# Where the weight buffers of the second expert stage lie, and which step lets the third expert's weights be fetched

## The chip, the cores and the metric

The kernel runs on one core of a Trainium2 chip. The metric is device microseconds of one launch; the span of a profile is the time from its first to its last instruction on that core.

## The reference

A two-layer model: each layer is a mixer followed by a mixture of experts. The changed code is the expert part and the seam between it and the mixer in front of it.

```python
DEPTH = 2
MOE_EXPERTS = 32          # 4 groups of 8
MOE_TOP_K = 2
MOE_FF = D_MODEL // 2     # 512, D_MODEL = 1024

for l in range(DEPTH):
    ...                                        # norm, modulation, mixer: even for l = 0, odd for l = 1
    x = x + mod_l[2][:, None] * y_l            # out projection of the mixer, residual
    h2_l = rms_norm(x, norm_w[l, 1]) * (1.0 + mod_l[4][:, None]) + mod_l[3][:, None]
    ...                                        # l = 0: 256 context tokens and 512 others; l = 1: 512
    y2 = hierarchical_moe(h2, wg, bg, we, be, w1, w3, w2)

# hierarchical_moe: a group, then the two best experts of it for each token; for each expert
#   y = (silu(x @ w1[e]) * (x @ w3[e])) @ w2[e]
# scaled by its gate and added up for each token
```

Every expert has three float32 matrices of 2 MB: w1 and w3 (1024x512) and w2 (512x1024). The 32 experts of a stage are 192 MB, and the two stages read 384 MB.

## The kernel before

The order on the core is: even mixer, expert stage l = 0 (768 tokens, "first stage"), odd mixer, expert stage l = 1 (512 tokens, "second stage"), final norm.

**The seam.** `mix_out` (L663) does the out projection of the mixer in 128-token tiles, four for l = 1 and six for l = 0. For each tile it loads the residual (tile `oxr`, SP's queue), runs two groups of matmuls into `po`, adds, stores `xmid`, computes the normed rows, stores them to DRAM as `h2d` (POOL's queue), and routes the tile's tokens. The last matmul of tile n's out projection is kept as `s.marks[n]` (in the order in which tiles are done), the second residual load as `s.oxr1`. Behind the last tile the routing builds the tables `ixm`, which say for each expert which rows to gather. The residual tiles and the routing's work tiles (pools `mob` and `mow`) are memory that is in use until those tables are done.

**An expert stage.** `moe` (L890) handles expert e in iteration e and e + 1: POOL gathers its token rows (`hga`, and `hgb` for an overflow block), PE transposes them (`xt`), multiplies by w1 and w3 (`pa`, 16 matmuls of the program, 32 in the trace), transposes the gated product (`gt`) and multiplies by w2 (`ya`); POOL scatters the result to `yd`. For the overflow block there are `pb` and `yb`; PE reads a flag of the expert from memory (`values_load` of `fl`, L1003, a TENSOR_LOAD) and branches to the real block or to one short matmul with zeros. All 32 flags of a stage are read by PE's own queue, at places that the scheduler picks.

**The weights.** All weight loads go through `wdma` (L950) in one chain on SP's queue, 1 MB each. I number these pieces of a stage from 0: pieces 0 to 3 are w2 of experts 0 and 1; 4 to 7, 8 to 11 and 12 to 15 are w1 and w3 of experts 0, 1 and 2; 16 to 19 those of expert 3, 20 to 23 of expert 4; then six for each expert, beginning with w2 of expert 2 (24 and 25), of expert 3 (30 and 31), and so on, so that w2 of expert 8 begins with piece 60. SP's queue runs in order: a piece that waits holds all that stands behind it, residual loads too.

Two things hold a piece. The first is its memory: `load13` takes buffers of 2 MB (two pieces each) from seven in turn, `load2` takes its two pieces from a ring of four 1 MB buffers, which w2 of the expert before the last has to leave first (its `yb` is the last reader). The seven buffers are pools that are opened at the right end of memory, `rb` first, then `ra`, and what they overlie depends on that. In the built program of the second stage one of the seven, byte 81,888 of each partition, overlies the routing's work tiles (`mob`, `mow`); the six from 98,272 on overlie memory that the mixer itself has left by then. The one over the routing is the first in turn. The second thing is pacing: the list `ahead` says for the first pieces which `marks` entry each has to wait for, and the two pieces after the list wait for `gathers[3]`, the fourth gather.

Of the kernel before, what the change touches and what calls it, by code (L numbers as in the profile page):

```python
# [8 lines left out]
F32 = mybir.dt.float32  # L9
# [73 lines left out]
class Kern:  # L83
# [806 lines left out]
    def moe(s, l):  # L890
# [6 lines left out]
        yv = [s.yd[l][:2 * ntok].rearrange("t (h n) -> (t h) n", h=m) for m in (2, 4)]  # L897
        with ExitStack() as es:
            rb = es.enter_context(s.pool(f"ringb{l}", bufs=(2, 3)[l], side="right"))
            ra = es.enter_context(s.pool(f"ringa{l}", bufs=4, side="right"))  # L900
            rc = es.enter_context(s.pool(f"ringc{l}", side="right")) if l == 0 else rb
            mp = es.enter_context(s.pool(f"moe{l}"))
            wk = es.enter_context(s.pool(f"moew{l}", bufs=2))
            pst = es.enter_context(s.pool(f"moet{l}", bufs=2, psum=True))
# [11 lines left out]
            scat, turn, chain, gathers = [], [0], [], []  # L916


            ahead = [-1, -1, -2, -2] + [[0, 0, 1, 1, 2, 2, 3, 3, 5, 5], [0, 0, 0, 1, 1, 1, 2, 2, 3, 3]][l]

            def columns(e):

# [22 lines left out]
            def at(wv, e, k0, k1):  # L945
                if isinstance(e, int):
                    return wv[e, :, k0:k1]
                return wv[bass.ds(e, 1), :, k0:k1].rearrange("a p k n -> (a p) k n")

            def wdma(e, dst, src):  # L950
                x = nc.sync.dma_start(dst, src)
                if isinstance(e, int):
                    if chain:
                        s.pace(x, chain[-1], False)

                    if len(chain) < len(ahead):
                        if ahead[len(chain)] >= 0:
                            s.pace(x, s.marks[ahead[len(chain)]])
                        elif ahead[len(chain)] == -2:
                            s.pace(x, s.oxr1, True)  # L960
                    elif len(chain) < len(ahead) + 2:
                        s.pace(x, gathers[3])
                    chain.append(x)

            def load13(e):
                r = []
                for a in range(2):
                    t = (ra, ra, ra, ra, rb, rb, rc)[turn[0] % 7].tile([128, 2, 4, 512], F32, name="mw")
                    turn[0] += 1
                    for i, wv in enumerate((w1, w3)):  # L970
                        wdma(e, t[:, i], at(wv, e, 4 * a, 4 * a + 4))
                    r.append(t)
                return r
# [55 lines left out]
            def gxpose(g):  # L1029
                t = pst.tile([128, 512], F32, tag="t", name="gt")  # L1030
                for c in range(3):
                    nc.tensor.transpose(t[:, c * 128:(c + 1) * 128], g[:, c * 128:(c + 1) * 128], s.ident)  # L1032
                gT = wk.tile([128, 384], F32, name="gT")
                nc.vector.tensor_copy(gT, t[:, :384])
                return gT
# [34 lines left out]
            if l == 1:  # L1070

                m5a, m5b = mp.tile([128, 512], F32, name="m5a"), mp.tile([128, 256], F32, name="m5b")
                for t, m in ((m5a, 2), (m5b, 4)):
                    n = D // m
                    for i in range(m):
                        src = s.modd[1][2][4 + 2 * (i * n // 512):5 + 2 * (i * n // 512), i * n % 512:i * n % 512 + n]
                        s.pace(nc.gpsimd.dma_start(t[128 // m * i:128 // m * (i + 1)], src.to_broadcast([128 // m, n])), gathers[3], False)
            w2t = [load2(0), load2(1)]
            w13 = [load13(0), load13(1), load13(2)]
            xs = {0: [xpose(0, 0), xpose(0, 1)]}  # L1080
            g, pb, yb, gT = {}, {}, {}, {}
            for e in range(NE + 1):
                if e < NE:
                    if e + 2 < NE:
                        gather(e + 2, columns(e + 2))
                    if 0 < e < NE - 2:
                        w13.append(load13(e + 2))
                    if e > 1:
                        w2t.append(load2(e))
# [26 lines left out]

            if l == 1:
                big = lambda pool: pool.tile([128, 2, 4, 512], F32, name="mw").rearrange("p a b c -> p (a b c)")
                fin = s.final_load(big(ra), big(ra))
            else:  # L1120
                s.vraw = s.vload(0)

            with tc.For_i(0, nov, 1) as o:  # L1123
                cols = []
                for ix, gt in s.R["otab"]:
                    c = wk.tile([128, 2], I32, name="ocol")
                    nc.vector.tensor_copy(c[:, 0:1], ix[:, 0, bass.ds(o, 1)])
                    nc.vector.tensor_copy(c[:, 1:2], ix[:, 1, bass.ds(o, 1)])
                    g = wk.tile([128, 1], F32, name="ogate")
                    nc.vector.tensor_copy(g, gt[:, bass.ds(o, 1)])  # L1130
                    cols.append((c[:, 0:1], c[:, 1:2], g))
                e = nc.values_load(s.R["oi"][0:1, bass.ds(o, 1)], engines=[mybir.EngineType.SP], min_val=0, max_val=NE - 1)
                gather(NE, cols)
                w, wd = load13(e), load2(e)
                pa = up_a(w, xpose(NE, 0))
                xb, p = xpose(NE, 1), pbt()
                up_b(p, w, xb)
                gg = wk.tile([128, 384], F32, name="gg")
                gate(gg, pa, 0, 256)
                gate(gg, p, 256, 128)  # L1140
                t = gxpose(gg)
                down_a(wd, t, cols)
                p = ybt()
                down_b(p, wd, t)
                tail_b(p, cols)
# [322 lines left out]
```

## Time and profile before

| | us |
|---|---|
| median of 3 runs | 2089.74 |
| lowest and highest | 2088.02, 2091.30 |
| the profiled execution | 2089.85 |
| its span | 2088.1 |
| first expert stage, from its first gather | about 510 to 1010 |
| odd mixer | about 1010 to 1465 |
| out projection and routing of l = 1 | about 1465 to 1534 |
| second expert stage | about 1534 to 2045 |
| final norm | about 2045 to 2088 |

PE is busy 1802.3 us of the span (86%) and the weight loads, 384 transfers of 1024 KB, make up most of the 567.73 MB that the DMA engines move. The mean granted clock is 0.963. Shares over the whole span mix stages with different limits, so the stretches have to be read one by one: in the page's slices the DMA row is at 9 in both expert stages and low in the mixers and at the seam between them.

### The profile page before, as it was taken

Reading aid. Unit: us, or ns where it says so; the run is one execution under the profiler, and the core shown is the slowest. Engines: PE = TensorE matmul, PEld = TensorE weight load, DVE = VectorE, ACT = ScalarE, POOL = GpSimd, SP = SyncE. Lnnn points to the kernel's source line nnn. Section 1 sums busy time; section 2 is a strip of 40 time slices with the busy share of each in tenths; the row PEclk is TensorE's granted clock in tenths of the full one; section 3 lists DMA queues with packets and bytes.
Section 4 is the critical chain, followed back from the end, with each engine's and each line's share of the span. In section 5 each row is a group of like instructions: output and inputs, shape, how many; then the busy total and the mean of one; then the engine's idle time right before and its main releaser. Section 6 shows DMA issues by size and latency. Waiting matters only on the chain. (4 is left out here: it accounts for less than half of the span.)

```text
span 2088.1 us, 26462 instructions
## 1 busy us (share of the span) xinstructions
PE 1802.3 (86%) x10109; PEld 843.4 (40%) x10109; DVE 869.0 (42%) x1823; ACT 563.3 (27%) x929; POOL 353.3 (17%) x400
## 2 busy tenths in 40 slices
PE   5999999996989999888589999999959888888882
PEld 2564444453333333233234566556533333333320
DVE  5476455578111111111273796777851212111113
ACT  4355356511111111111243554654210000000000
POOL 2000000013322222211230000000132223222213
PEclk9999999998999999999889999999969999999996
DMA  9515556574999999999773130110469999999996
GB/s 318 202 54 194 193 173 206 183 284 165 410 410 363 412 412 410 410 412 414 298 256 81 41 81 24 61 61 21 175 244 409 411 410 410 410 411 410 410 397 231
DMA packets 168718, 567.73 MB, mean 272 GB/s; under 512 B 21702, under 2 KB 69311, under 8 KB 130659
## 3 DMA queue, kind: packets, MB, share of 16 engines
q1 hardware_dynamic: 145632, 523.88, 65.1%
q0 software_dynamic: 22640, 41.30, 5.6%
q8 instruction: 127, 2.08, 0.4%
q14 instruction: 45, 0.36, 0.0%
q10 hardware_dynamic: 274, 0.10, 0.0%
HBM read 554.59 MB, written 39.91 MB: 285 GB/s over the span
## 5 line engine op out<-in xcount | busy, mean ns | idle before, releaser
L144 PE MATMUL pa<-mw,xa 128*64 128x512 f32 x2048 | 537.0, 608 | 28.9 <-DMA mw<-in_moe_w 24.6
L144 PE MATMUL ya<-mw,gT 128*64 128x512 f32 x1024 | 283.8, 602 | 2.3 <-DMA mw<-in_moe_w 1.5
L144 PEld LDWEIGHTS pa<-mw,xa 128*64 128x64 f32 x2048 | 158.4, 139 | 284.1 <-issue 277.4
L144 PE MATMUL px<-hTh,wsh 128*128 128x512 f16 (+1 forms) x672 | 227.1, 339 | 7.5 <-DVE t L438 2.8
L144 PE MATMUL px<-hTl,wsh 128*128 128x512 f16 (+1 forms) x672 | 227.3, 338 | 2.7 <-DVE hTl L348 2.6
L144 PE MATMUL px<-hTh,wsl 128*128 128x512 f16 (+1 forms) x672 | 226.9, 338 | 0.0
L144 PEld LDWEIGHTS <-wsh 128*128 128x128 f16 x1344 | 131.2, 98 | 118.9 <-issue 22.8
L1027 DVE TENSOR_TENSOR gg<-gg,pa 128x256 f32<-128x256 f32 x64 | 26.9, 420 | 332.3 <-ACT gg L1026 332.3
L937 POOL DMA_INDIRECT yd<-sb,ixm x64 | 66.0, 1032 | 583.3 <-DVE sb L1062 293.7
L144 PEld LDWEIGHTS ya<-mw,gT 128*64 128x64 f32 x1024 | 79.3, 136 | 114.4 <-issue 98.3
L1027 DVE TENSOR_TENSOR gg<-gg,pb 128x128 f32<-128x128 f32 x64 | 18.4, 288 | 254.5 <-ACT gg L1026 252.3
L1026 ACT ACTIVATE gg<-pa 128x256 f32<-128x256 f32 x64 | 24.6, 384 | 360.5 <-PE pa L144 360.5
L1026 ACT ACTIVATE gg<-pb 128x128 f32<-128x128 f32 x64 | 17.7, 277 | 277.3 <-PE pb L144 277.3
L138 DVE SCALAR_TENSOR_TENSOR wsl<-w,wsh 128x2048 f16<-128x2048 f32 x34 | 77.8, 2289 | 35.4 <-ACT wsh L135 31.5
L1032 PE MATMUL gt<-cca,gg 128*128 128x128 f32 x192 | 46.5, 306 | 50.5 <-DVE gg L1027 50.5
L144 PEld LDWEIGHTS <-wsl 128*128 128x128 f16 x672 | 66.3, 99 | 51.4 <-issue 6.0
L927 POOL DMA_INDIRECT hga<-h2d,ixm x64 | 66.9, 1045 | 101.7 <-PE xt L987 75.7
L1032 PEld LDWEIGHTS gt<-cca,gg 128*128 128x128 f32 x192 | 21.5, 141 | 147.5 <-DVE gg L1027 98.8
L144 PE MATMUL adaps<-adaw,cT 128*32 128x512 f32 x384 | 75.7, 633 | 4.5 <-DMA adaw<-in_ada_w 3.4
L992 ACT ACTIVATE xa<-xt 128x512 f32<-128x512 f32 x64 | 38.2, 597 | 140.3 <-PE xt L987 137.9
L937 POOL DMA_INDIRECT yd<-sa,ixm x64 | 64.3, 1005 | 69.2 <-ACT sa L1046 31.3
L144 PE MATMUL pv<-wsh,hTh 128*128 128x512 f16 (+1 forms) x192 | 69.0, 360 | 5.8 <-ACT hTh L1227 5.8
(391 smaller groups left out, 2761.5 us busy)
## 6 DMA issues: line engine op xcount, KB each, us to landing
mw<-in_moe_w SPq DMA_DIRECT2D x384, 1024.0 KB
adaw<-in_ada_w SPq DMA_DIRECT2D x40, 1024.0 KB
w<-in_od_w_in SPq DMA_DIRECT2D x32, 512.0 KB
adaw<-in_ada_w SPq DMA_DIRECT2D x16, 512.0 KB
w<-in_ev_w_in SPq DMA_DIRECT2D x8, 1024.0 KB
cy<-yd SPq DMA_DIRECT2D x12, 512.0 KB
xmid<-oxr POOLq DMA_DIRECT2D x10, 512.0 KB
h2d<-ohp POOLq DMA_DIRECT2D x10, 512.0 KB
```

What stands on the lines that cost most here:

```text
L138: i = s.nc.vector.scalar_tensor_tensor(lo, v, WS, hi, op0=ALU.mult, op1=ALU.subtract)
L144: return s.nc.tensor.matmul(ps, lhsT, rhs, start=first, stop=last)
L927: i = nc.gpsimd.indirect_dma_start(out=hg[e % NG][g], out_offset=None, in_=hv[g], in_offset=bass.IndirectOffsetOnAxis(ap=cols[g][0], axis= ...
L937: i = nc.gpsimd.indirect_dma_start(out=yv[g], out_offset=bass.IndirectOffsetOnAxis(ap=cols[g][1], axis=0), in_=yt, in_offset=None, bounds_ ...
L992: nc.scalar.activation(x, v, AF.Copy)
L1026: nc.scalar.activation(g[:, c0:c0 + n], p[:, :n], AF.Silu)
L1027: nc.vector.tensor_tensor(g[:, c0:c0 + n], g[:, c0:c0 + n], p[:, n:2 * n], op=ALU.mult)
L1032: nc.tensor.transpose(t[:, c * 128:(c + 1) * 128], g[:, c * 128:(c + 1) * 128], s.ident)
```

## The change

In the second stage the buffers are split otherwise: `ra` has three, `rb` three, and a pool `rc` of its own holds the seventh. `rc` is opened last, lies at byte 81,888 over the routing's tiles, and comes last in turn; the six buffers before it, 12 pieces, lie on memory that the mixer has left. The final loads take `rb` in place of `ra`.

The list `ahead` grows by two entries in both stages. In the first stage pieces 14 and 15 wait for `marks[5]`, the last out-projection matmul, where they waited for the fourth gather, and pieces 16 and 17 now wait for that gather. In the second stage pieces 10 to 15 wait for `marks[3]`, the last out-projection matmul (10 and 11 waited for `marks[2]`, 14 and 15 for the gather), and 16 and 17 for the gather. So all of w1 and w3 of expert 2 is paced by the out projection.

```diff
             rb = es.enter_context(s.pool(f"ringb{l}", bufs=(2, 3)[l], side="right"))
-            ra = es.enter_context(s.pool(f"ringa{l}", bufs=4, side="right"))
-            rc = es.enter_context(s.pool(f"ringc{l}", side="right")) if l == 0 else rb
+            ra = es.enter_context(s.pool(f"ringa{l}", bufs=(4, 3)[l], side="right"))
+
+            rc = es.enter_context(s.pool(f"ringc{l}", side="right"))
+            ring = [ra] * (4, 3)[l] + [rb] * (2, 3)[l] + [rc]
...
-            ahead = [-1, -1, -2, -2] + [[0, 0, 1, 1, 2, 2, 3, 3, 5, 5], [0, 0, 0, 1, 1, 1, 2, 2, 3, 3]][l]
+            ahead = [-1, -1, -2, -2] + [[0, 0, 1, 1, 2, 2, 3, 3, 5, 5, 5, 5], [0, 0, 0, 1, 1, 1, 3, 3, 3, 3, 3, 3]][l]
...
-                    t = (ra, ra, ra, ra, rb, rb, rc)[turn[0] % 7].tile([128, 2, 4, 512], F32, name="mw")
+                    t = ring[turn[0] % 7].tile([128, 2, 4, 512], F32, name="mw")
...
-                fin = s.final_load(big(ra), big(ra))
+                fin = s.final_load(big(rb), big(rb))
```

SP's queue at the seam to the second stage, before; `in_moe_w2` are pieces 0 to 3, and `mw_13321` is the first buffer of expert 0:

```order
L678 DMA oxr_12649<-xres_66 128x1024
L678 DMA oxr_12678<-xres_66 128x1024
L951 DMA mw_13317<-in_moe_w2 128x2x1024
L951 DMA mw_13318<-in_moe_w2 128x2x1024
L678 DMA oxr_12937<-xres_66 128x1024
L678 DMA oxr_13080<-xres_66 128x1024
L951 DMA mw_13321<-in_moe_w1 128x2048
L951 DMA mw_13321<-in_moe_w3 128x2048
L951 DMA mw_13324<-in_moe_w1 128x2048
```

and after, where line numbers are two higher and `mw_13324` is that first buffer:

```order
L678 DMA oxr_12649<-xres_66 128x1024
L678 DMA oxr_12678<-xres_66 128x1024
L953 DMA mw_13320<-in_moe_w2 128x2x1024
L953 DMA mw_13321<-in_moe_w2 128x2x1024
L678 DMA oxr_12937<-xres_66 128x1024
L953 DMA mw_13324<-in_moe_w1 128x2048
L953 DMA mw_13324<-in_moe_w3 128x2048
L678 DMA oxr_13080<-xres_66 128x1024
L953 DMA mw_13327<-in_moe_w1 128x2048
```

Pieces 4 and 5 have moved ahead of the fourth residual load; the pieces behind follow it directly.

The scheduler also moves PE's flag reads. PE's queue at the start of the second stage before, from the transposes of expert 0's overflow rows on:

```order
L987 MATMUL xt<-cca,hgb_13276 128x128 x2
L1003 TENSOR_LOAD fl_13243
L1003 ISA x2
...
L144 MATMUL ov<-o_14570,osl 128x48 x5
L144 MATMUL pa<-mw,xa 64x512 x8
L144 MATMUL ov<-o_14570,osl 128x48 x3
```

and after:

```order
L989 MATMUL xt<-cca,hgb_13279 128x128 x2
L144 MATMUL pa<-mw,xa 64x512
L1006 COMPARE_AND_BRANCH
L144 MATMUL pb<-mw,xb 32x256 x32
...
L144 MATMUL pa<-mw,xa 64x512 x15
L989 MATMUL xt<-cca,hga_13282 128x128 x4
```

Before, nine flag reads stand between those transposes and the first `pa`; after, none. PE's queue further on in the second stage after, at `gt` of expert 7 and `yb` of expert 6, where before no flag read stands:

```order
L1034 MATMUL gt<-cca,gg 128x128 x3
L989 MATMUL xt<-cca,hga_13282 128x128 x4
L1005 TENSOR_LOAD fl_13243
L1005 ISA x2
...
L144 MATMUL pa<-mw,xa 64x512 x7
L144 MATMUL ya<-mw,gT 64x512 x4
L144 MATMUL pa<-mw,xa 64x512
L1034 MATMUL gt<-cca,gg 128x128
L1006 COMPARE_AND_BRANCH
L144 MATMUL yb<-mw,gT 32x256 x16
```

Of the 32 flag reads of the second stage, 18 stood ahead of the first `pb` and the other 14 within experts 0 to 3; after, 9 stand ahead of `pa` of expert 1 and 23 between `gt` of expert 4 and `yb` of expert 6. The first stage has that second order in both kernels, with its 23 reads placed a little otherwise.

## Rows read from the trace of the kernel before

**Rows 1.** The page, slices: mean busy tenths of the DMA engines, 40 slices of 52.2 us.

```profile
DMA  9515556574999999999773130110469999999996
```

**Rows 2.** Stretches: engines' busy us, granted clock, DMA share, GB/s.

```profile
1500.00:1535.00 35.00, 21.80 (x126) 14.51 (x124) 28.59 (x106) 3.88 (x12) 7.48 (x16) 0.78 0.15 61
1535.00:1560.00 25.00, 11.86 (x43) 5.94 (x45) 7.52 (x21) 1.03 (x3) 12.64 (x16) 0.56 0.99 364
```

**Rows 3.** Timeline of SP's DMA issues, second stage: start, length, line, transfer, count.

```profile
1483.94 9.85 SPq L678 DMA_DIRECT2D oxr<-xres  x2
1534.61 164.51 SPq L951 DMA_DIRECT2D mw<-in_moe_w  x66
```

**Rows 4.** Waits of SP's queue, 1465 to 1540: total us, times, longest.

```profile
SPq L951 <- DVE ixm L804: 40.7, 1, 40.7
```

**Rows 5.** Waits of PE, 1750 to 2040.

```profile
PE pa L144 <- DMA mw<-in_moe_w: 13.4, 12, 2.3
```

**Rows 6.** PE timeline, transposes of experts 14 and 30: start, us, idle before, releaser.

```profile
1765.94 0.33 PE L1032 MATMUL gt<-cca,gg 128*128 128x128 f32 x1 [0.93 <-DVE gg L1027]
...
2024.61 0.33 PE L1032 MATMUL gt<-cca,gg 128*128 128x128 f32 x1 [0.93 <-DVE gg L1027]
```

**Rows 7.** POOL timeline, first and fourth gather of each stage.

```profile
510.48 1.13 POOL L927 DMA_INDIRECT hga<-h2d,ixm  x1 [3.72 <-DVE tum L802]
...
1534.07 1.10 POOL L927 DMA_INDIRECT hga<-h2d,ixm  x1 [5.94 <-issue]
1538.30 1.00 POOL L927 DMA_INDIRECT hgb<-h2d,ixm  x1 [0.30 <-issue]
```

**Rows 8.** PE timeline of the first stage's early experts.

```profile
513.82 1.11 PE L987 MATMUL xt<-cca,hga 128*128 128x128 f32 x4 [4.08 <-DMA hga<-h2d,ixm]
539.05 0.28 PE L144 MATMUL yb<-zero 128*128 128x256 bf16 x1
...
615.97 6.57 PE L144 MATMUL pa<-mw,xa 128*64 128x512 f32 x16 [3.96 <-issue]
622.47 3.66 PE L144 MATMUL pb<-mw,xb 128*32 128x256 f32 x64
635.06 3.65 PE L144 MATMUL pa<-mw,xa 128*64 128x512 f32 x16
648.87 0.28 PE L144 MATMUL yb<-zero 128*128 128x256 bf16 x1
```

**Rows 9.** PE timeline of the second stage's early experts.

```profile
1540.92 1.08 PE L987 MATMUL xt<-cca,hga 128*128 128x128 f32 x4 [7.51 <-DMA hga<-h2d,ixm]
1549.89 2.34 PE L144 MATMUL ov<-o,osl 128*128 128x48 f32 x10 [5.68 <-issue]
...
1609.02 3.66 PE L144 MATMUL pb<-mw,xb 128*32 128x256 f32 x64
...
1648.20 1.93 PE L144 MATMUL yb<-mw,gT 128*32 128x256 f32 x32
...
1678.94 0.28 PE L144 MATMUL yb<-zero 128*128 128x256 bf16 x1
```

**Rows 10.** Waits of SP's queue, 520 to 660, and a stretch inside it.

```profile
SPq L951 <- PE yb L144: 52.0, 4, 18.8
...
625.00:635.00 10.00, 9.79 (x66) 3.74 (x55) 1.66 (x4) 1.77 (x4) 1.44 (x2) 1.00 0.61 234
```

**Rows 11.** PE timeline, last out-projection matmul of each stage; a first-stage stretch behind it.

```profile
492.54 0.38 PE L144 MATMUL po<-wo01h,yTl 128*128 128x512 f16 x1
...
1515.93 0.38 PE L144 MATMUL po<-wo11h,oyTl 128*128 128x512 f16 x1
...
495.00:505.00 10.00, 2.41 (x20) 2.22 (x20) 8.45 (x14) 1.54 (x4) 4.86 (x12) 0.70 0.77 294
```

**Rows 12.** DVE and POOL timelines: the fourth tile's residual add, the last h2d store.

```profile
1510.53 0.69 DVE L688 TENSOR_TENSOR oxr<-oxr,po 128x512 f32<-128x512 f32 x1
...
1524.34 0.58 POOL L710 DMA_DIRECT2D h2d<-ohp  x1 [3.60 <-DVE r L745]
```

## The prediction

> **What bounds the kernel now.** I read the slices first, to find where the DMA engines are idle beside stages that live off them; then the seam to the second stage; then the end of that stage; then the start of the first stage, because it already has the order that the change gives to the second.
>
> The slices [rows 1] show DMA at 9 tenths in both expert stages and at 0 to 4 at the seam before the second. There the DMA engines are 0.15 busy from 1500 to 1535 and 0.99 from then on [rows 2]. The reason is in SP's queue: the pair of `oxr`, the third and fourth residual loads, ends at 1483.94 + 9.85 = 1493.8, and until 1534.61 SP issues nothing [rows 3], and its longest wait, 40.7 us, is for `ixm`, the routing's last table [rows 4]. Pieces 4 and 5 go to the one buffer that lies over the routing's tiles, and every later piece stands behind them.
>
> Whether these idle microseconds matter is decided at the stage's end. From 1750 to 2040 PE waits 12 times for weights before `pa` [rows 5]. Experts 14 and 30 are 2024.61 - 1765.94 = 258.7 us apart [rows 6], 16.17 us each, or 2.70 us for each of the six 1 MB pieces, gathers and scatters included. So the end is set by the weight stream, and what counts is how far that stream has come at the last moment at which it was held up. Before, it is held up only at the start: piece 4 begins about 1535.5 (issue plus some 0.9 us, an estimate), and piece 60 (w2 of expert 8) follows 56 x 2.70 = 151.2 us later, at 1686.7. Its memory is given free by `yb` of expert 6 at 1678.94 [rows 9], 7.8 us earlier, so PE holds nothing.
>
> **The change, second stage.** Twelve pieces, 12 x 2.70 = 32.4 us of stream, move to memory that is free, and go out from about 1484 on: two ahead of the fourth residual load, four behind it, six behind the last out-projection matmul at 1516.3 [rows 11]. All of them fit into the idle stretch: the last six need 16.2 us, until about 1533 to 1535. The pieces from 16 on wait for the fourth gather, issued at 1538.30 [rows 7]; with 3.3 us to land (below) they begin about 1542.6 instead of 1567.9 (1535.5 + 32.4). So the stream is 25.3 us ahead there. That is the upper bound of the gain.
>
> I do not take it, because the stream now meets PE. PE's side: the first gather is issued at 1534.07 as before [rows 7]. In the first stage, with few transfers beside it, the first transposes follow 513.82 - 510.48 = 3.3 us behind it [rows 7, 8]; in the second stage before, into the starting stream, 6.9 us (1540.92) [rows 9]. After, only the end of six early pieces is in the way: I take 1538.0, with 1537.4 and 1540.9 as the ends. The nine flag reads that cost PE 5.68 us ahead of expert 0 [rows 9] go, but 23 reads now stand between experts 4 and 8, as they do in the first stage. There they are not hidden: a group of six left PE empty for 3.96 us [rows 8], which is 0.66 each, as the 5.68 for nine are 0.63. From the first transposes to `yb` of expert 6 the first stage takes 648.87 - 513.82 = 135.1 us [rows 8]. Two overflow blocks of 3.66 us were real there (one of them in [rows 8]) instead of some 0.28; in the second stage one `pb` of 3.66 and one `yb` of 1.93 are real in that stretch [rows 9]. That makes 135.1 - 6.8 + 3.4 + 1.6 = 133.3 us, so `yb` of expert 6 comes at 1538.0 + 133.3 = 1671.3, and piece 60 begins at about 1672.5. The stream alone would have been there at 1542.6 + 44 x 2.70 = 1661.4: it stands idle for about 11 us in all, in one or two places, as the first stage's did for 3.9 us between 625 and 635 (share 0.61) [rows 10], where SP waited for `yb` up to 18.8 us [rows 10]. From piece 60 on the stream runs through as before: PE's own pace is 14.5 us an expert (two experts from 1648.20 to 1678.94, less 1.65 for a real `yb` [rows 9]) against the stream's 16.17, so PE comes to wait for weights again. So the end comes 1686.7 - 1672.5 = 14.2 us earlier.
>
> What goes with this: the fourth residual load stands behind 2 MB more. Issued at 1493.5 [rows 3], with 5.4 us for those and some 3 of its own (the gather's), it lands by 1502, 8 us ahead of its add at 1510.53 [rows 12]; that costs nothing. The last `h2d` store, issued at 1524.34 [rows 12], gets six pieces beside it and has 9.7 us until the first gather. The first stage already does this: it has a DMA share of 0.77 from 495 to 505, and its way from the last out-projection matmul (492.9) to the first gather is 17.6 us; the second stage's with idle DMA engines is 17.8 (1516.3 to 1534.07) [rows 7, 11]. So I take nothing for the crowding, with +3.5 us (the gather's 6.9 against 3.3) as its upper end. The Trainium skill, DMA: Bandwidth & Descriptors, "Issuing engines are not separate DMA queues", speaks against the change here: transfers started from any engine share the same 16 DMA engines and interleave, so early weights slow the stores and the gather; by it the gain would be some 10.7 in place of 14.2, and the gather's two times agree with it, the two 17.6 and 17.8 do not show it. The final loads take `rb`, whose buffers are free long before SP reaches them behind w2 of expert 31: nothing.
>
> **The change, first stage.** Two pieces, 5.4 us, leave the time behind the fourth gather for the idle stretch before it. But that stage's stream is held by `yb` at expert 6 already [rows 10], and PE's work up to there is the same, 23 flag reads included. So what is gained at the start is waited for there: I take 0, from -2 to +2 for the other places of the reads; -5.4 would need PE not to hold the stream.
>
> **Sum.** 2089.85 - 14.2 - 0 = 2075.6 us, against the profiled execution (span 2088.1 and 1.75 around it), which stands within 0.2 us of the median 2089.74. Its own range: the gather's landing -0.6 to +2.9, the reads and the half clock that followed one group (16 matmuls of `pa` in 6.57 us in place of 3.65 [rows 8]) -3 to +3, the first stage -2 to +2: 2070 to 2082.
>
> **The rivals.** (1) The reads hide behind work, and the stream runs through: 25.3 us, 2064.5. For it: the 14 reads that stood within experts 0 to 3 before left no gap like 5.68 there that I found. Against it: the 3.96 us gap in the same order [rows 8]. (2) The crowding or late buffers make the first gather 6 to 9 us late: 2082 to 2085; against it, the first stage's 17.6 us. (3) The early pieces still wait for the routing, because something the program lays on the six buffers is read until then: 2089.9, no change. Against it: the order of SP's queue, where pieces 4 and 5 stand ahead of a residual load that the routing itself needs; that order could not run if they waited for the routing. (4) Slower: PE's clock. It was 0.56 of full speed from 1535 to 1560 [rows 2], behind a stretch with little work, and a group of reads brought it down again in the first stage. At the half level (1.2 in place of 2.4 GHz) an expert's 32 matmuls of `pa` and 16 of `ya` take 3 x 6.57 in place of 3 x 3.65 us, 8.8 more. With the reads in five groups, three experts at that level cost 26.3 us, and since `yb` of expert 6 then comes at 1697.6, past 1686.7, the whole would take 2101.9; from 1.6 experts on the gain is gone. Against it: the first stage, with as many reads, lost 2.9 us in the one place that rows 8 show. The Trainium skill, TensorE: Matmul & The Clock Gate, "HAM oscillation — how this bites in real kernels", describes such a loop, in which waits between bursts of matmuls throttle each next burst anew; rows 8 show it once, for 16 matmuls.
>
> **How the numbers follow.** The forecast 0.62, (1) 0.20, (2) 0.08, (3) 0.05, (4) 0.05. A measurement of this kernel can tell about 0.2%, 4.2 us, from no change. Forecast, (1) and (2) all are faster by more: 0.90; (3) is the same: 0.05; (4) slower: 0.05. The range takes the forecast's own range and rival (1): 2064 to 2082.
>
> **What would show it.** In the changed kernel's profile SP should issue two weight pieces at about 1484, and DMA be busy from 1516 to 1534; the first `xt` of the second stage stand near 1538, `yb` of expert 6 near 1671, and the DMA share fall below 1 somewhere between 1620 and 1675, then stay at 1 until PE's last experts, which again wait for weights. If the share stays at 1 throughout, rival (1) is right; if `xt` comes after 1541, (2). The forecast is wrong if PE comes to `yb` of expert 6 at another time than computed, for the gain hangs on that alone.

## The result and the profile after

The changed kernel takes 2068.15 us (median; 2067.45 to 2068.79) against 2089.71 for the kernel before on the same chip: a ratio of 0.9899, with a 95% interval of 0.9887 to 0.9911, or 21.6 us less. The forecast was 14.2 us less, and rival 1 (the stream runs through) 25.3 us less. The profiled execution took 2068.66 us with a span of 2066.9, so 21.2 us of the 21.6 are in the trace that is read here.

The slices of the page after answer to [rows 1]; here the DMA row alone; behind the valley of the odd mixer it climbs by 0, 5, 8, 9, where before it went 0, 4, 6, 9:

```profile
DMA  9515555575999999999792221120589999999996
```

The same two windows as in [rows 2], then five of 10 us where the prediction looked for a dip (columns: us, PE busy, PEld, DVE, ACT, POOL, PEclk, DMA share, GB/s):

```profile
1500.00:1535.00 35.00, 19.56 (x107) 12.67 (x106) 28.87 (x103) 3.83 (x13) 9.86 (x19) 0.73 0.83 331
1535.00:1560.00 25.00, 24.08 (x106) 9.47 (x108) 6.78 (x21) 4.32 (x8) 14.22 (x17) 0.90 0.91 342
1630.00:1640.00 10.00, 7.57 (x35) 3.61 (x34) 2.29 (x5) 1.58 (x3) 5.70 (x6) 0.83 1.02 403
1640.00:1650.00 10.00, 9.56 (x47) 3.44 (x43) 2.32 (x5) 1.26 (x3) 1.74 (x2) 1.00 0.76 280
1650.00:1660.00 10.00, 6.10 (x16) 1.91 (x16) 0.42 (x1) 0.00 (x0) 2.35 (x3) 0.66 1.00 383
1660.00:1670.00 10.00, 9.07 (x43) 3.28 (x41) 1.92 (x5) 0.66 (x2) 1.03 (x1) 1.00 0.62 237
1680.00:2010.00 330.00, 284.71 (x1364) 103.19 (x1362) 61.61 (x130) 26.82 (x64) 79.17 (x78) 1.00 1.02 410
```

The DMA engines are at 0.83 where they were at 0.15 before. Then the stream falls to 0.76 and 0.62 in two places, and from 1680 on it is full: the picture that the forecast drew, and not rival 1's.

SP's queue after, which answers to [rows 3], and its waits from 1465 to 1545, which answer to [rows 4]:

```profile
1480.29 0.34 SPq L678 DMA_DIRECT2D oxr<-xres  x1
1480.68 0.90 SPq L953 DMA_DIRECT2D mw<-in_moe_w  x2
1492.41 0.33 SPq L678 DMA_DIRECT2D oxr<-xres  x1
1492.79 208.24 SPq L953 DMA_DIRECT2D mw<-in_moe_w  x71
```

```profile
SPq L953 <- DMA hgb<-h2d,ixm: 21.0, 1, 21.0
SPq L953 <- PE po L144: 17.5, 1, 17.5
```

Two pieces go out between the third and the fourth residual load. The 40.7 us for `ixm` are gone; in their place SP waits for the last out-projection matmul and then for the gather, as the list `ahead` says.

The second stage's start and the way to `yb` of expert 6, which answer to [rows 7, 9]; first POOL's first gather, then PE's timeline (start, us, and in brackets the idle time before and what ended it):

```profile
1530.74 1.09 POOL L929 DMA_INDIRECT hga<-h2d,ixm  x1 [5.94 <-DVE tum L802]
```

```profile
1533.79 1.09 PE L989 MATMUL xt<-cca,hga 128*128 128x128 f32 x4 [3.70 <-DMA hga<-h2d,ixm]
...
1635.21 5.35 PE L144 MATMUL pa<-mw,xa 128*64 128x512 f32 x16 [1.88 <-issue]
...
1653.90 6.42 PE L144 MATMUL pa<-mw,xa 128*64 128x512 f32 x16 [3.94 <-issue]
...
1667.08 0.28 PE L144 MATMUL yb<-zero 128*128 128x256 bf16 x1
...
2011.49 3.19 PE L144 MATMUL pa<-mw,xa 128*64 128x512 f32 x13 [1.39 <-DMA mw<-in_moe_w]
...
2017.89 0.33 PE L1034 MATMUL gt<-cca,gg 128*128 128x128 f32 x1 [0.93 <-DVE gg L1029]
```

PE stands empty for 1.88 and 3.94 us ahead of `pa` with nothing in the profile that it waits for; those are its flag reads: in the trace, TENSOR_LOADs of `fl` on PE's queue start at 1633.74 and 1634.42 in the first gap and at 1650.30, 1650.98, 1651.66, 1652.40 and 1653.08 in the second. At the end it still waits for weights (the row of 2011.49), over 1750 to 2020 as here, which answers to [rows 5]:

```profile
PE pa L144 <- DMA mw<-in_moe_w: 9.3, 9, 1.9
```

In the first stage, which answers to [rows 7, 8], the gather starts 0.87 us later than before and `yb` of expert 6 comes 1.84 us earlier:

```profile
511.35 1.12 POOL L929 DMA_INDIRECT hga<-h2d,ixm  x1 [3.72 <-DVE tum L802]
```

```profile
631.04 5.85 PE L144 MATMUL pa<-mw,xa 128*64 128x512 f32 x16 [3.91 <-issue]
...
647.03 0.28 PE L144 MATMUL yb<-zero 128*128 128x256 bf16 x1
```

**The ledger.** I cut the program at POOL's first gather of each stage and at PE's `gt` of the last expert in each stage. Those `gt` are, before, and then after for the first stage (the second stage's is the row of 2017.89 above):

```profile
1009.43 0.33 PE L1032 MATMUL gt<-cca,gg 128*128 128x128 f32 x1 [0.93 <-DVE gg L1027]
...
2040.04 0.33 PE L1032 MATMUL gt<-cca,gg 128*128 128x128 f32 x1 [0.93 <-DVE gg L1027]
```

```profile
1005.74 0.33 PE L1034 MATMUL gt<-cca,gg 128*128 128x128 f32 x1 [0.93 <-DVE gg L1029]
```

From first gather to last `gt`, the first stage went from 498.95 to 494.39 us (-4.56) and the second from 505.97 to 487.15 (-18.82). The work ahead of the first gather got 0.87 longer, the odd mixer with its routing 0.37 (524.63 to 525.00), and the tail 0.96 (48.02 to 48.98). The sum is -21.2. These last three are smaller than the scatter: over the thirteen profiles of this study the first gather starts between 507.5 and 511.4, and the odd mixer with its routing takes 522.0 to 526.4. (The three longest of these mixers, 525.9 to 526.4, belong to e5, e8 and e9, the changed kernel with the reads spread in both stages; whether that is chance stays open.)

### The profile page after: what moved, and what is told of

Its sections match the earlier page's. It is cut to its first block, busy times and chain, and to the rows that moved or that the text cites. A ratio compares the mean times of both kernels' runs of the same rounds, so it can differ in the third digit from the quotient of the medians.

```text
span 2066.9 us, 26460 instructions
## 1 busy us (share of the span) xinstructions
PE 1801.0 (87%) x10109; PEld 841.6 (41%) x10109; DVE 868.0 (42%) x1823; ACT 562.9 (27%) x929; POOL 353.7 (17%) x400
## 5 line engine op out<-in xcount | busy, mean ns | idle before, releaser
L1029 DVE TENSOR_TENSOR gg<-gg,pb 128x128 f32<-128x128 f32 x64 | 18.4, 288 | 250.8 <-ACT gg L1028 250.8
L1036 DVE COPY gT<-gt 128x384 f32<-128x384 f32 x64 | 35.4, 554 | 115.2 <-PE gt L1034 115.2
L1034 PEld LDWEIGHTS gt<-cca,gg 128*128 128x128 f32 x192 | 21.2, 140 | 137.6 <-DVE gg L1029 86.9
## 6 DMA issues: line engine op xcount, KB each, us to landing
mw<-in_moe_w SPq DMA_DIRECT2D x384, 1024.0 KB, 18.7
```

The lines of the kernel that those rows point to most:

```text
L1029: nc.vector.tensor_tensor(g[:, c0:c0 + n], g[:, c0:c0 + n], p[:, n:2 * n], op=ALU.mult)
```

## The experiments

Theory 1 was the prediction's own mechanism: in the changed kernel PE's flag reads between experts 4 and 8 hold the weight stream, so the end of each stage follows from PE's `yb` and not from how early the first pieces go. The rival took the early pieces themselves (their number and their pace) for the whole effect, with PE holding nothing. For each kernel I read the length of the two stages, from first gather to the last expert's `gt`, and in brackets that from first gather to `yb` of expert 6:

| kernel | first stage, us | second stage, us |
|---|---|---|
| before | 498.95 (138.4) | 505.97 (144.9) |
| after | 494.39 (135.7) | 487.15 (136.3) |
| after, once more | 494.9 (135.2) | 487.2 (136.4) |
| e1: before, first stage's two entries | 494.2 (135.3) | 505.6 (145.0) |
| e2: after without those | 498.0 (138.2) | 487.3 (136.5) |
| e3: after, second stage's old list | 493.2 (134.0) | 487.4 (133.4) |
| e4: after, reads spread in the second stage | 494.1 (135.5) | 481.9 (127.7) |
| e5, e9: after, reads spread in both | 491.3, 490.9 (129.5, 129.0) | 481.1, 481.1 (127.5, 127.3) |
| e6: e4 with the second stage's old list | 495.0 (135.9) | 485.7 (130.9) |
| e7: before, reads spread in both | 494.6 (131.8) | 505.7 (144.5) |
| e8: e5 with the first stage's old list | 494.5 (130.5) | 481.9 (127.7) |
| f1: before, second stage's new list | 498.4 (138.8) | 506.0 (144.9) |

Where a stage has the same edits, its length comes back within 0.4 us in the second stage (before, e1, e7, f1: 505.6 to 506.0; after, a1, e2: 487.1 to 487.3) and within 1.7 in the first (494.4, 494.9, 493.2, 494.1, 495.0 for after, its repeat, e3, e4, e6). The parts outside the stages scatter by 4 us, so the stages tell more than the medians.

**e1, the first stage's part alone**, on the kernel before:

```diff
-            ahead = [-1, -1, -2, -2] + [[0, 0, 1, 1, 2, 2, 3, 3, 5, 5], [0, 0, 0, 1, 1, 1, 2, 2, 3, 3]][l]
+            ahead = [-1, -1, -2, -2] + [[0, 0, 1, 1, 2, 2, 3, 3, 5, 5, 5, 5], [0, 0, 0, 1, 1, 1, 2, 2, 3, 3]][l]
```

> The kernel before with the two added entries of the first stage's pacing list alone (pieces 14 and 15 wait for the last out-projection matmul). In the changed kernel everything behind the first stage lies 3.2 us earlier. Theory 1: this comes from the first stage's part of the change, so here about 2086.5 us, with the second stage as before and only shifted. Rival: the first stage's pieces gain nothing, because PE holds the stream at expert 6 as it did, and the 3.2 us have another source: about 2089.7 us.

2085.56 against 2088.44, a ratio of 0.9982 (0.9970 to 0.9995): 2.9 us less, and 4.8 less in the first stage itself. The prediction's 0 for this part was wrong.

**e2, the changed kernel without that part**, so that the second stage's part stands alone:

```diff
-            ahead = [-1, -1, -2, -2] + [[0, 0, 1, 1, 2, 2, 3, 3, 5, 5, 5, 5], ...
+            ahead = [-1, -1, -2, -2] + [[0, 0, 1, 1, 2, 2, 3, 3, 5, 5], ...
```

> The changed kernel with the first stage's pacing list of before: the second stage's part alone. Theory 1: the parts add up, so 2068.2 + 3.2 = about 2071.4 us. Rival: the second stage gives all of it and the shift comes from elsewhere: about 2068.2 us.

2070.05, a ratio of 0.9907 (0.9887 to 0.9927): 18.4 us less. With e1's 2.9 that is 21.3 of the 21.6, so the two parts add up, and the second stage's part is worth 18.7 in its own stage (505.97 to 487.3). The interval of the ratio, some 2065 to 2073 us, holds the expectation of theory 1 and of the rival both; it is the lengths of the stages, 498.0 and 487.3, that decide for the sum of two parts.

**e3, the changed kernel with the second stage's old list**, so that pieces 14 and 15 wait for the gather again:

```diff
-            ahead = ... [0, 0, 0, 1, 1, 1, 3, 3, 3, 3, 3, 3]][l]
+            ahead = ... [0, 0, 0, 1, 1, 1, 2, 2, 3, 3]][l]
```

> The changed kernel with the second stage's old pacing list: pieces 10 and 11 wait for the third tile's last matmul, 14 and 15 for the fourth gather, 16 and 17 for their memory. Two pieces, 5.4 us of stream, start behind the gather again. Theory 1: the stream is held by PE up to yb of expert 6 and has some 8 us of idle time to lose before that, so nothing changes: 2067 to 2069 us. Rival: the stream's lead is what counts at every piece, and the third expert's pacing is worth its 5.4 us: about 2073.6 us.

2068.75, a ratio of 0.9903 (0.9882 to 0.9925), the same as the changed kernel; the stage takes 487.4 in place of 487.15. So the time is the one that theory 1 expected. The test is not a clean one, though: the reads stand otherwise here too, and PE comes to `yb` of expert 6 133.4 us after the gather in place of 136.3. Had the stream's lead over the kernel before followed that `yb` alone, it would have been 19.0 us where 66 MB have moved (an estimate: the 16.1 of the changed kernel, counted below, and the 2.9 us that PE is earlier); by the bytes moved it is 16.9. So some 2 us that the later start cost may be hidden in the equal lengths. The dips are still there, one of them at another place. Windows and the `yb` of expert 6 in e3:

```profile
1630.00:1640.00 10.00, 5.97 (x21) 2.06 (x22) 0.42 (x1) 0.22 (x2) 2.62 (x3) 0.83 1.01 393
1640.00:1650.00 10.00, 9.60 (x48) 3.62 (x46) 2.74 (x6) 1.14 (x3) 2.37 (x3) 1.00 0.82 308
```

```profile
1659.38 0.28 PE L144 MATMUL yb<-zero 128*128 128x256 bf16 x1
```

**e4, the flag reads of the second stage spread out**, on the changed kernel: PE's read of expert e's flag is placed behind the transposes of that expert's rows, one read for each expert from the third on, so that no group of reads forms. No work is left out.

```diff
                     i = nc.tensor.transpose(t[:, c * 128:(c + 1) * 128], hg[e % NG][g][:, c * 128:(c + 1) * 128], s.ident)
+                    xlast[e] = i
...
-                    flag[e] = nc.values_load(s.R["fl"][0:1, e:e + 1], engines=[mybir.EngineType.PE], min_val=0, max_val=1)
+                    ld, vs = nc.values_load_multi_w_load_instructions(s.R["fl"][0:1, e:e + 1], engines=[mybir.EngineType.PE], min_val=0, max_val=1)
+                    if l == 1 and e > 1:
+                        s.pace(ld[0], xlast[e], False)
+                    flag[e] = vs[0]
```

> The changed kernel with PE's flag reads of the second stage placed one to an expert, behind the transposes of that expert, in place of 23 between experts 4 and 8. Theory 1: the reads hold PE, PE holds the stream; without the bunch yb of expert 6 comes some 13 us earlier, the stream keeps the lead of about 26 us that it has at its start, and the DMA share has no dip between 1600 and 1680: 2058 to 2062 us. Rival: the dips come from something else that the early pieces meet (memory, gathers), and the reads cost the same wherever they stand: 2067 to 2069 us. A third way: one read an expert lengthens every expert so that PE becomes the bound: above 2068 us.

2060.34, a ratio of 0.9859 (0.9837 to 0.9881): 28.1 us less than before, 8.4 less than e3 and 9.7 less than e2 on the same chip. The second stage takes 481.9 in place of 487.15, 5.2 less; what the medians show above that lies outside the stages, where the profiles scatter. This is the run that decides. PE's waits from the first gather to `yb` of expert 6, first of the changed kernel (1535 to 1668), then of e4 (1535 to 1665):

```profile
PE pa L144 <- issue: 5.8, 2, 3.9
...
PE gt L1034 <- DVE gg L1029: 0.9, 1, 0.9
```

```profile
PE gt L1038 <- DVE gg L1033: 1.9, 2, 0.9
PE xt L989 <- ACT xa L995: 1.5, 2, 0.7
PE ov L144 <- issue: 0.4, 2, 0.3
...
PE pa L144 <- issue: 0.4, 1, 0.4
```

Of the 5.8 us ahead of `pa` 0.4 are left. In e4's timeline a single read costs 0.35 us, `pa` behind it runs at full clock (3.65 in place of 6.42 and 5.35), and `yb` of expert 6 comes 8.6 us sooner after the gather (127.7 in place of 136.3); theory 1 had said some 13. In the windows the dips are smaller but not gone: theory 1 had expected none and a lead that stays near 26 us, and one dip of 0.88 is left.

```profile
1644.85 3.65 PE L144 MATMUL pa<-mw,xa 128*64 128x512 f32 x16 [0.35 <-issue]
...
1655.41 0.28 PE L144 MATMUL yb<-zero 128*128 128x256 bf16 x1
```

```profile
1640.00:1650.00 10.00, 8.75 (x42) 3.29 (x44) 2.41 (x5) 0.87 (x2) 4.09 (x4) 1.00 0.88 324
1650.00:1660.00 10.00, 7.91 (x40) 3.03 (x38) 2.54 (x5) 0.98 (x2) 2.07 (x3) 1.00 1.01 416
1660.00:1670.00 10.00, 9.11 (x41) 3.04 (x40) 0.72 (x3) 0.66 (x2) 1.99 (x2) 1.00 1.03 407
```

**e5, the reads spread in both stages** (e4 with `if e > 1:`):

> The changed kernel with PE's flag reads placed one to an expert in both stages (the run before this one did so in the second alone and took 28.1 us less than the kernel before, where the changed kernel took 21.6 less). Theory 1 (bunched reads hold PE, PE holds the stream): the first stage loses its dip of about 4 us between experts 6 and 8 too, so about 31 us less than before, 2058.5 us. Rival: the first stage's dip has another cause: 28 us less, about 2061.5 us.

2058.70, a ratio of 0.9852 (0.9830 to 0.9874): 30.0 us less than before. The first stage shortens once more, from 494.1 to 491.3.

**e6, e4 with the second stage's old list** (the edit of e3 on e4):

> Reads one to an expert in the second stage, and the second stage's pacing list of before (pieces 14 and 15 behind the fourth gather). With bunched reads that list cost nothing. Theory 1: it cost nothing because PE held the stream behind it; with that hold gone the two pieces cost most of their 5.4 us, so 23 to 25 us less than the kernel before, about 2065.5 us. Rival: the third expert's pacing is worth nothing in any case, because the first experts' weights are there and the stream catches up elsewhere: 28 us less, about 2061.5 us.

2066.31, a ratio of 0.9888 (0.9866 to 0.9910): 22.4 us less than before, where theory 1 had said 23 to 25 and the rival 28. With the reads out of the way the later start does count: the stage takes 485.7 in place of 481.9, where with the reads in groups (e3 against the changed kernel) the difference was 0.3. The same edit costs next to nothing or 3.8 us of the stage, depending on whether PE holds the stream later; how near to nothing stays open by what was said at e3. Windows of e6, then of e4, at the stage's start:

```profile
1510.00:1530.00 20.00, 8.98 (x51) 6.99 (x49) 15.99 (x59) 1.94 (x6) 4.88 (x12) 0.66 0.68 263
1530.00:1545.00 15.00, 10.92 (x37) 3.53 (x38) 8.22 (x26) 2.35 (x4) 11.85 (x15) 0.66 0.55 186
```

```profile
1510.00:1530.00 20.00, 5.42 (x35) 4.33 (x33) 17.54 (x59) 2.14 (x7) 6.90 (x14) 0.66 0.94 371
1530.00:1545.00 15.00, 13.52 (x55) 5.28 (x55) 6.32 (x19) 3.14 (x5) 12.25 (x16) 0.77 0.75 259
```

**e7, the kernel before with the reads spread in both stages** (the edit of e5 on the kernel before):

> The kernel before with reads one to an expert in both stages, nothing else. Theory 1: in its second stage the weight stream never waits for PE, so the reads' places are worth nothing there; in its first stage the dip goes: about 4 us less than before in all, 2085.5 us, and all of that ahead of the odd mixer. Rival: the reads' places are worth the same 8 us in the second stage as in the changed kernel, and 12 us less in all: 2077.5 us.

2084.52 against 2088.69, a ratio of 0.9982 (0.9970 to 0.9994), all of it in the first stage (494.6). The second stage stays at 505.7: there, before the change, PE did not hold the stream, as the prediction said. The first stage's stretch of [rows 10] (share 0.61 from 625 to 635) is full in e7:

```profile
620.00:630.00 10.00, 8.50 (x42) 3.39 (x41) 1.89 (x4) 1.67 (x3) 3.96 (x4) 1.00 1.01 413
630.00:640.00 10.00, 9.84 (x94) 3.81 (x89) 0.29 (x1) 0.40 (x2) 0.13 (x1) 1.00 1.03 414
```

**e8, e5 with the first stage's old list**, to price the two pieces there with the reads out of the way:

> Reads one to an expert in both stages of the changed kernel, with the first stage's pacing list of before. Theory 1: in the first stage the two early pieces' 5.4 us are lost again at piece 24, which waits for yb of expert 0, and only about 1 us of them stays; what the first stage gained in the changed kernel came from the other places of its flag reads. So 30 us less than before, within 1.5 us of the same kernel with the new list. Rival: the early pieces are worth their 5.4 us once PE holds nothing: some 5 us slower than the same kernel with the new list.

2061.19, a ratio of 0.9867 (0.9846 to 0.9887). The first stage takes 494.55 in place of e5's 491.28: 3.3 us for the two pieces, 2.5 in the medians. Theory 1 had expected at most 1.5 and the rival 5, so neither holds as written; with the reads spread the pieces do count, for more than half of their 5.4 us of stream. Reads alone (e7) are worth 4.3 in this stage, both together 7.7.

**f1, the second stage's new list alone**, on the kernel before, with the buffers where they were:

```diff
-            ahead = ... [0, 0, 0, 1, 1, 1, 2, 2, 3, 3]][l]
+            ahead = ... [0, 0, 0, 1, 1, 1, 3, 3, 3, 3, 3, 3]][l]
```

> The kernel before with the second stage's new pacing list alone; the buffer over the routing's tiles is still the first in turn. Theory 1: the place of that buffer is what held the pieces, so the list changes nothing, pieces from 4 on go out behind the routing's last table: 0 to 1 us from the kernel before. Rival: part of the gain is the list's, and pieces go out ahead of the routing: 5 us or more less than before.

2088.28 against 2088.82, a ratio of 0.9997 (0.9986 to 1.0008): no difference. SP's queue shows why, its timeline first, then its waits:

```profile
1480.29 10.37 SPq L678 DMA_DIRECT2D oxr<-xres  x2
1531.46 28.66 SPq L951 DMA_DIRECT2D mw<-in_moe_w  x16
```

```profile
SPq L951 <- DVE ixm L804: 40.7, 1, 40.7
```

The queue still stands for 40.7 us behind the buffer over the routing. Of the change's two halves in this stage, the place of the buffers did the work that the stage's length shows; the pace added 0.3 us to it (e3 against the changed kernel), and without the place it did nothing (f1).

**The changed kernel once more, and e5 once more** (labels a1 and e9), side by side on one chip:

> The changed kernel once more, beside the next one on the same chip: 20 to 22 us less than the kernel before.

> The changed kernel with reads one to an expert in both stages, once more, beside the changed kernel on the same chip. Theory 1: the sum of the two stages is 30 us less than before and 9 less than the changed kernel. Rival: the difference to the changed kernel was one of chips, below 4 us here.

2066.89, a ratio of 0.9890 (0.9870 to 0.9910), and 2058.03, a ratio of 0.9862 (0.9837 to 0.9887). The kernel with the change and the spread reads is faster than both, by 8.9 us against the changed kernel in these medians and by 10.2 in the lengths of the two stages (494.92 + 487.21 against 490.91 + 481.05).

## Why the prediction was right and where it was off

**Right: the bound and the place.** The weight stream set the end before and sets it after; the pieces went out where the SP queue was read to free them; and the stream is held by PE near expert 6. SP issued two pieces at 1480.68 (forecast about 1484), DMA was busy at the seam, and the share fell to 0.76 from 1640 to 1650 and to 0.62 from 1660 to 1670 (forecast: below 1 somewhere within 1620 to 1675). PE waits for weights again at the end. The first transposes, 1533.79 (forecast near 1538), and `yb` of expert 6, 1667.08 (near 1671), stand earlier by the clock, but 3.3 us of that is the earlier start of the whole stage. f1 shows that the buffer's place, not the list, was what held the queue.

**Right, and to the tenth by luck: PE's way.** From the first transposes to `yb` of expert 6 the prediction carried 133.3 us over from the first stage, with two overflow blocks exchanged. It is 1667.08 - 1533.79 = 133.3. The basis was sound: one observation from a stage whose reads stand in the same order. That it fits to a tenth is luck, for the same way, from the transposes on, takes 130.5 us in e3, where the reads stand a little otherwise, and 132.4 in the changed kernel's own first stage (647.03 - 514.59).

**Right: the crowding costs nothing.** The last out-projection matmul before the gather starts at 1512.61 after, and 1512.61 + 0.38 to the first gather at 1530.74 is 17.75 us; before it was 17.76 [rows 7, 11]. The gather's data reach PE in 1533.79 - 1530.74 = 3.05 us, against 6.85 before [rows 7, 9]; the prediction took 3.9. The Trainium skill, DMA: Bandwidth & Descriptors, "Issuing engines are not separate DMA queues", says that transfers from any engine run on the same 16 DMA engines and interleave; taken as a rule for the time, that has the early weights slow the stores and the gather. The gather's two times fit that rule, slow where it met the starting stream; the way to the gather, 17.75 and 17.76, shows no cost at a DMA share of 0.83. A slower store could still be hidden in it, because what the gather waits for last is DVE's `tum` and not the store (the row of 1530.74). In all thirteen profiles that way is 17.73 to 17.76 us; the gather takes 6.75 to 6.85 us in the four where the stream starts together with it (before, e1, e7, f1) and 2.98 to 3.18 in the other nine, where all but about 1 MB of the pieces that are let go ahead of it have moved by then.

**Right: rival 4 did not come.** PE's clock fell to half behind the two gaps, as 5.35 and 6.42 us in place of 3.65 show (4.5 us together), and was back with the next matmuls (PEclk 0.66 from 1650 to 1660, then 1.00). The Trainium skill, TensorE: Matmul & The Clock Gate, "HAM oscillation — how this bites in real kernels", describes a loop, in which a wait between bursts of matmuls throttles the clock each time; here it ended after one group of 16 matmuls each time.

**Off: the first stage, forecast 0, measured -4.6.** The steps that failed were "what is gained at the start is waited for there" and, under it, "PE's work up to there is the same". PE's way to `yb` of expert 6 became 2.7 us shorter (138.4 to 135.7): two groups of reads, with gaps of 3.96 us [rows 8] and of 2.04 before, became one with a gap of 3.91 (the row of 631.04 above). The other 1.9 us came behind that `yb`. The prediction bounded "other places of the reads" at 2 us; but with the longer list the scheduler lays the reads otherwise. e1 shows that the list alone does this (494.2, and 135.3 to that `yb`). How much of it in the changed kernel is the reads and how much the pieces stays open: e7 and e8 price both (4.3 and 3.3 us) only with the reads spread.

**Off: the second stage, forecast 14.2, measured 18.8.** Four terms, in us:

- The gather and `yb`: +0.9. The time from the gather to the transposes was 3.05, not 3.9.
- The stream before came to piece 60 later than computed: by the bytes that SP's transfers had moved it was there at 1689.2, not at 1686.7, which is +2.5. Its start was right (piece 4's first bytes move at 1535.56, forecast 1535.5). The step that failed is "56 x 2.70": 2.70 us a piece is the rate of the stage's second half, and [rows 2] show 364 GB/s from 1535 to 1560 where the full stream moves 410. I had the row and used the other rate.
- Getting started again behind the dip: -1.5. I count the megabytes that have moved from piece 4 on, so that piece 60 begins at 56 MB and 66 MB is the end of piece 69. The stream after is at 66 MB 27.7 us after piece 60 could start (1667.08 + 1.2), where the stream before took 26.2 for the same ten pieces. The lead falls from 17.6 to 16.1 by that; at 180 MB it is 16.4.
- The last weights: +2.4. PE's last wait for weights ends at 2011.49 after (row above) and, in the same place, at 2033.65 before:

```profile
2033.65 3.19 PE L144 MATMUL pa<-mw,xa 128*64 128x512 f32 x13 [1.39 <-DMA mw<-in_moe_w]
```

That is 22.2 us earlier, though the bytes of the stream are 19.7 to 20.0 earlier there. When PE may go on, 184.8 MB, counted so, have moved before, but 184.06 after: 0.7 MB, which is 2 us. In the trace each piece sets 16 marks (semaphore updates), as many as there are DMA engines, and PE goes on 0.13 us behind the last mark of expert 31's last w1 or w3 piece (2033.52 before, 2011.36 after). On the mean that piece's marks stand 8.1 us ahead of the last one before and 5.7 after; the difference, 2.4 us, is this term. It stood nowhere in the prediction.

The sum is 14.2 + 0.9 + 2.5 - 1.5 + 0.3 + 2.4 = 18.8, where 0.3 is the lead that grows between 66 and 180 MB. The terms that were missed on the gaining side outweigh the one on the other, and the first stage's 4.6 has the same sign. The forecast's own range, 2070 to 2082, missed the 2068.15 by 1.9 us; the range that was given, 2064 to 2082, held because it reached to rival 1, whose mechanism did not come with this order of reads. That is luck: the time lies 3.7 us from rival 1 and 7.5 from the forecast, and what brought it there are terms that neither of the two had.

**Rival 1, by bytes.** With times counted from the first gather of the stage and megabytes from piece 4, the changed kernel's stream is 25.4 us ahead of the one before at 32 MB (forecast 25.3), 24.2 at 48 MB and 16.1 at 66 MB. So 9.3 us go at the dips, where the forecast had 11.1. With the reads spread (e4) it is 25.3, 24.5 and 22.7: 2.6 us go even then, in part at the dip of 0.88. The reads in groups thus cost 6.6 us of the stream, of which 5.2 are left at the stage's end. Rival 1 had its mechanism right, but not for this order of reads: with the reads spread the second stage gains 24.1 (e4) to 24.9 us (e5).

## What to carry to other kernels

Where a stage lives off one stream, ask at which moment the stream was last held up: work ahead of that moment is free, and the same edit is worth little or most of its length according to it (0.3 us in e3, 3.8 of 5.4 in e6). Before pacing a queue, look at which memory its head waits for (f1). And when a change lets a stream start early, price what else will now hold it: here 5.8 us of flag reads in groups and the half clock behind them, where spreading the reads gained the second stage 0.3 us before the change (e7) and 5.2 after (e4).

## What the runs showed of the hardware

**In a long stream the 16 marks of a piece drift apart, and an idle gap draws them together.** In the kernel before, the marks of one piece, from first to last, span about 5.4 us at 1650, 8.2 at 1696 and 15.6 for the last w1 or w3 piece of the second stage. In the changed kernel they span 2.0 us for the piece that ends at 1667.0, 0.2 for the next one at 1672.2, right behind the dip, and then again more and more, to 14.1 for that last piece. PE waits for the last mark, so what counts at the stage's end is how far the marks stand ahead of it on the mean: 8.1, 7.7, 7.8 and 7.6 us in the kernel before, e1, f1 and e7, all with a stream that ran through from its start; 5.7, 5.5 and 5.5 in the changed kernel, e2 and the changed kernel's second run, whose streams stood still just ahead of `yb` of expert 6; 6.5 to 7.3 in e3 to e6, e8 and e9, with smaller or earlier dips. The megabytes moved by the time PE gets expert 31's last weights go with it: 184.7 to 184.8 for the first four, 184.4 to 184.7 for the last six, 184.0 to 184.1 for the three between. So a stall of the stream gives some 2 us of itself back at the end. That the gap is the cause is read from how these runs line up; no run put a gap in on its own.

**A short row of register reads can bring PE's clock down, and does not always.** The prediction had this for one gap of 3.96 us. A gap of 1.88 us was enough in the changed kernel: the 16 `pa` matmuls behind it took 5.35 us in place of 3.65, with the granted clock at 0.83 from 1630 to 1640. Behind 3.94 us they took 6.42, behind 3.91 us 5.85, and behind the 0.35 us of a single read (e4) 3.65. But behind gaps of 2.01 us in e3's second stage (at 1619) and 2.03 in e2's first (at 601) the granted clock stayed at 1.00, while behind 2.04 us at the same place of the kernel before it fell to half for 3.4 us. So a group of reads costs up to 2.9 us more behind its gap than the gap shows (6.57 against 3.65 [rows 8]); what decides between the two outcomes near 2 us is not shown.
